# Decoder layer with sparse attention: the first head's bias tile on GpSimd's queue, and filling products that go on past a projection's end

## The chip, the cores and the metric

The kernel runs on one core of one Trainium2 chip. A core has a matrix engine (TensorE, PE in the profile), a vector engine (VectorE, DVE), an activation engine (ScalarE, ACT), GpSimd (POOL) and SyncE (SP). Each works through its own list of instructions in order, and waits for others through semaphores. SP, ACT and POOL also issue transfers (DMA). The metric is the device time of one execution in microseconds (us); lower is better.

## The reference, cut to what matters

One decoder layer on 512 tokens of width 2048 in float32: an attention with three branches, then a gated feed-forward part.

```python
proj = h @ w_in                       # q (16 heads), kc vc ks vs kw vw (4 groups), gates
s_c = q . kcc + bias_c                # compressed keys (31 blocks)
s   = q . kg  + bias                  # selected blocks (with 512 tokens: all of them)
s_w = q . kwb + bias_w                # window of 512
p   = masked_softmax(...)             # each branch
o   = gates0 * o_c + gates1 * o_s + gates2 * o_w
return o.reshape(S, 16 * 128) @ w_out
...
h = h + nsa_mixer(rmsnorm(h), ...)
h = h + swiglu(rmsnorm(h), ffn_w_in, ffn_w_out)
return rmsnorm(h, final_norm_g)
```

The bias depends on the distance of query and key and on the head.

## The kernel before, in words

Every float32 operand is split into a rounded high part and a rest, and each product is three TensorE instructions (`three`, lines 264 to 267). Weights come in granules of 512 KB: a load on SP's queue into one of three `raw` buffers, then a split, high part on ScalarE (line 95), rest on VectorE (line 96), into one of four pairs of buffers. `W.take` hands out the next granule and keeps loads and splits ahead of use.

Three stages follow each other: the first projections with the compression (lines 348 to 625), the attention over 16 heads (lines 628 to 864), and the output projection with the feed-forward part. The change touches the attention.

**The order of one head.** The order of all work is written by hand; each engine gets its instructions in the order in which the code issues them. For each head `h` and block `t` of 128 query tokens, `scores` issues the score products into the one score tile `sc` (three banks of the accumulator memory) and then, per branch, a VectorE instruction that adds the bias and finds the maximum (line 773) and a ScalarE exponential (line 775). The bias of the two long branches is read from the tile `TB[h]`, 128 x 512, one buffer. `finish` scales the result on VectorE. `turn` transposes a piece on TensorE (line 797) into one of two `pt` banks, from which ScalarE and VectorE split it (lines 290, 291), and `values` multiplies it with the values. Blocks are taken from 3 down to 0. Blocks 3 and 2 of the next head are scored at the end of a head.

**The filling products.** TensorE would often wait for the softmax. Between the pieces of a head, `pump(h, step)` therefore issues products of the projections that later heads need: the generator `dense` (lines 711 to 719) goes through queries of two heads (`qpair`), keys and values of the next group (`kpair`, `vpair`), and at the end four pieces of the output projection (`partial`). Each yield of a number is one unit: 650 planned nanoseconds. A projection has 32 units of six (`vpair`) or three instructions, a `partial` 24 of six instructions. It accumulates in two tiles `proj` out of two buffers, so the next projection's first units write where the one before has been read out. After its last unit a projection issues what is left of its read-out, counts itself in `done["n"]`, and yields `None`.

`pump` runs the generator until the planned time reaches a goal that grows with the head and step: one projection of 20,800 planned ns per head up to head 13, and 18,300 per head from there. A head has steps 0 to 11. `drain_to(h + 1)` in heads 0 to 12, between steps 9 and 10, runs it on until the projection that the next head needs is done.

**The first head.** Head 0 has nothing before it, so its blocks 3 and 2 are scored ahead of the loop. The lines are:

```python
load_bias(0)
pump(-1, 9.7)
scores(0, 3)
pump(-1, 10.5)
scores(0, 2)
finish(0, 3)
pump(-1, 11.2)
```

The tiles of the attention lie in memory that the stage before has released. So `TB[0]` and the tiles `P[t]`, whose first columns GpSimd clears (line 635), can be written only when the last readers there are done. The bias comes from `d_u`, a table in device memory that is complete long before. Later heads call `load_bias(h + 1)` within head `h`.

## Time and profile before

| | |
|---|---|
| median of 3 runs | 2159.72 us (2158.61 to 2160.09) |
| profiled execution, its own time | 2158.44 us |
| its span, first to last instruction | 2156.7 us |
| busy in the span: PE / DVE / ACT / POOL | 2136.3 / 1580.3 / 927.9 / 52.8 us |
| granted TensorE clock | 0.998 of full speed |
| attention, about | 196 to 735 us of the span |

The profile is one execution, recorded by the hardware. "Idle before" is the time that an engine stood still before an instruction, with what released it behind the arrow. Matmuls are pipelined: one of 512 columns is shown with 0.39 us, but the next starts some 0.23 us later, so TensorE's instructions overlap in the listing, and a stop shorter than that overlap does not show as idle time. PEld are the weight loads of TensorE. A line number in the profile can be that of a helper: lines 265 to 267 are all products, told apart by their tiles (`proj` filling products, `s` scores, `o` values, `pt` transposes).

### The profile page before, as it was taken

Reading aid. Unit: us, or ns where it says so; the run is one execution under the profiler, and the core shown is the slowest. Engines: PE = TensorE matmul, PEld = TensorE weight load, DVE = VectorE, ACT = ScalarE, POOL = GpSimd, SP = SyncE. Lnnn points to the kernel's source line nnn. Section 1 sums busy time; section 2 is a strip of 40 time slices with the busy share of each in tenths; the row PEclk is TensorE's granted clock in tenths of the full one; section 3 lists DMA queues with packets and bytes.
Section 4 is the critical chain, followed back from the end, with each engine's and each line's share of the span. In section 5 each row is a group of like instructions: output and inputs, shape, how many; then the busy total and the mean of one; then the engine's idle time right before and its main releaser. Section 6 shows DMA issues by size and latency. Waiting matters only on the chain.

```text
span 2156.7 us, 37078 instructions
## 1 busy us (share of the span) xinstructions
PE 2136.3 (99%) x15081; PEld 1983.8 (92%) x15081; DVE 1580.3 (73%) x2616; ACT 927.9 (43%) x1433; POOL 52.8 (2%) x107
## 2 busy tenths in 40 slices
PE   9999999999999999999999999999999999999998
PEld 7898898988989888899999999999999888989996
DVE  5565666665665446898888888888888787877785
ACT  5343454444444224343434434343443454444343
POOL 1000000000000000000000000000000000001000
PEclk9999999999999999999999999999999999999999
DMA  7554322322353543344344434344434686878894
GB/s 227 174 156 138 88 91 82 98 88 84 98 205 103 213 140 107 118 136 129 120 126 128 128 119 126 121 124 128 135 116 131 240 287 215 289 276 308 312 333 143
DMA packets 242727, 344.01 MB, mean 160 GB/s; under 512 B 13259, under 2 KB 179195, under 8 KB 241916
## 3 DMA queue, kind: packets, MB, share of 16 engines
q1 hardware_dynamic: 228412, 272.62, 40.1%
q0 software_dynamic: 12240, 64.82, 7.7%
q10 hardware_dynamic: 1904, 4.20, 0.5%
q8 instruction: 118, 1.93, 0.4%
q14 instruction: 53, 0.43, 0.1%
HBM read 298.50 MB, written 48.34 MB: 161 GB/s over the span
## 4 chain that ended last, share of the span: by engine, by line
PE 97%; DVE 1%; ACT 1%; DMA 1%; issue 0%; SPq 0%; ACTq 0%; DVEq 0%
PE f L266 19%; PE f L267 19%; PE f L265 19%; PE proj L265 8%; PE proj L267 8%; PE proj L266 8%; PE pt L797 2%; PE pp L265 1%; PE pp L266 1%; PE pp L267 1%; PE o L266 1%; PE o L267 1%; PE s L265 1%; PE o L265 1%; PE po L267 1%; PE po L265 1%
## 5 line engine op out<-in xcount | busy, mean ns | idle before, releaser
L96 DVE TENSOR_TENSOR wlo<-raw,whi 128x1024 fp32r<-128x1024 f32 (+1 forms) x226 | 272.3, 1208 | 127.7 <-ACT whi L95 126.2
L95 ACT ACTIVATE whi<-raw 128x1024 fp32r<-128x1024 f32 (+1 forms) x226 | 234.5, 1041 | 222.2 <-DVE raw L954 119.6
L954 DVE TENSOR_TENSOR tlo<-tt,thi 128x1536 fp32r<-128x1536 f32 (+2 forms) x135 | 197.1, 1460 | 110.2 <-ACT thi L1056 88.9
L265 PE MATMUL f<-hn_h,whi 128*128 128x256 f32 x984 | 271.7, 276 | 0.8 <-ACT E L1014 0.8
L267 PE MATMUL f<-hn_h,wlo 128*128 128x256 f32 x984 | 271.6, 276 | 0.0
L266 PE MATMUL f<-hn_l,whi 128*128 128x256 f32 x984 | 271.6, 276 | 0.0
L1051 ACT ACTIVATE whi<-raw 128x1024 fp32r<-128x1024 f32 x123 | 126.0, 1057 | 292.2 <-DVE raw L954 282.0
L265 PE MATMUL proj<-hn_h,whi 128*128 128x512 f32 x512 | 204.4, 399 | 0.5 <-ACT hn_h L400 0.5
L267 PE MATMUL proj<-hn_h,wlo 128*128 128x512 f32 x512 | 200.8, 392 | 0.0
L266 PE MATMUL proj<-hn_l,whi 128*128 128x512 f32 x512 | 199.9, 390 | 0.3 <-DVE hn_l L401 0.3
L265 PEld LDWEIGHTS f<-hn_h,whi 128*128 128x128 f32 x984 | 184.7, 188 | 1.2 <-ACT E L1014 1.2
L267 PEld LDWEIGHTS f<-hn_h,wlo 128*128 128x128 f32 x984 | 184.7, 188 | 0.0
L266 PEld LDWEIGHTS f<-hn_l,whi 128*128 128x128 f32 x984 | 184.7, 188 | 0.0
L1056 ACT ACTIVATE thi<-tt 128x1536 fp32r<-128x1536 f32 x82 | 121.9, 1487 | 84.2 <-PE f L266 84.2
L954 DVE TENSOR_TENSOR wlo<-raw,whi 128x1024 fp32r<-128x1024 f32 x123 | 147.0, 1223 | 0.0
L265 PE MATMUL proj<-whi,hn_h 128*128 128x256 f32 (+2 forms) x496 | 146.3, 295 | 0.0
L267 PE MATMUL proj<-whi,hn_l 128*128 128x256 f32 (+2 forms) x496 | 145.2, 293 | 0.0
L266 PE MATMUL proj<-wlo,hn_h 128*128 128x256 f32 (+2 forms) x496 | 145.0, 292 | 0.0
L291 DVE TENSOR_TENSOR ptl<-pt,pth 128x128 fp32r<-128x128 f32 (+3 forms) x128 | 62.3, 487 | 89.0 <-ACT pth L290 88.9
L267 PE MATMUL f<-whi,tlo 128*128 128x512 f32 x320 | 124.9, 390 | 0.6 <-DVE tlo L954 0.6
L266 PE MATMUL f<-wlo,thi 128*128 128x512 f32 x320 | 125.0, 391 | 0.0
L265 PE MATMUL f<-whi,thi 128*128 128x512 f32 x320 | 124.7, 390 | 0.0
(321 smaller groups left out, 6110.7 us busy)
## 6 DMA issues: line engine op xcount, KB each, us to landing
raw<-in_ffn_w_in SPq DMA_DIRECT2D x135, 512.0 KB, 3.7
raw<-in_ffn_w_out SPq DMA_DIRECT2D x88, 512.0 KB, 5.7
raw<-in_nsa_w_in SPq DMA_DIRECT2D x48, 512.0 KB, 3.8
rawx<-in_ffn_w_in SPq DMA_DIRECT2D x41, 512.0 KB, 4.8
raw<-in_nsa_w_out SPq DMA_DIRECT2D x32, 512.0 KB, 4.0
rawx<-d_a SPq DMA_DIRECT2D x31, 512.0 KB, 4.6
raw<-in_nsa_w_in SPq DMA_DIRECT2D x56, 256.0 KB, 3.4
ah<-d_s POOLq DMA_DIRECT2D x16, 896.0 KB, 6.9
```

Of the source, the lines that this page charges most:

```text
L95: self.nc.scalar.activation(hi[:, :n], src, AF.Copy)
L96: self.nc.vector.tensor_tensor(lo[:, :n], src, hi[:, :n].bitcast(F32), op=OP.subtract)
L265: mm(o, ah, bh, start=start, stop=False, skip_group_check=True)
L266: mm(o, ah, bl, start=False, stop=False, skip_group_check=True)
L267: mm(o, al, bh, start=False, stop=stop, skip_group_check=True)
L291: dve.tensor_tensor(lo, psum_ap, hi.bitcast(F32), op=OP.subtract)
L797: nc.tensor.transpose(pt[rows, 128 * (t - kt):128 * (t - kt + 1)], src, ident)
L954: dve.tensor_tensor(o, a, b, op=OP.subtract)
L1051: act(h, r, AF.Copy)
L1056: act(h, ttf, AF.Copy)
```

## The change

```diff
@@ -726,10 +726,10 @@ def pump(h, step):
             at = h + (step + 4) / STEPS
             goal = 20800 * min(at, 13) + 18300 * max(at - 13, 0)
             while done["ns"] < goal:
-                c = next(stream, None)
-                if c is None:
+                c = next(stream, "end")
+                if c == "end":
                     return
-                done["ns"] += c
+                done["ns"] += c or 0
@@ -744,7 +744,7 @@
         def load_bias(h):
             if h < H:
                 TB[h] = ap_.tile([128, S], F32, name="tb", bufs=1)
-                nc.sync.dma_start(TB[h], bass.AP(tensor=d_u.tensor, offset=d_u.offset + h * UL + 127,
+                (nc.sync if h else pool).dma_start(TB[h], bass.AP(tensor=d_u.tensor, offset=d_u.offset + h * UL + 127,
                                                  ap=[[H * UL - 1, 128], [1, S]]))
```

There are two edits. The bias tile of head 0 alone is loaded on GpSimd's queue instead of SP's; the other 15 stay on SP. And where a projection's end mark (`None`) comes up within a `pump`, the pump no longer returns: it goes on with the first units of the next projection until its goal is reached. It returns early only when all filling products are issued.

## The prediction

> **What bounds the kernel now.** I read the page first: span and engine shares, then busy time and clock by stretch of the attention, and last the order of time around each hole.

> ```profile
> span 2156.7 us, 37078 instructions
> PE 2136.3 (99%) x15081; PEld 1983.8 (92%) x15081; DVE 1580.3 (73%) x2616; ACT 927.9 (43%) x1433; POOL 52.8 (2%) x107
> ```

> ```profile
> core 0: us, PE busy (x) PEld busy (x) DVE busy (x) ACT busy (x) POOL busy (x), PEclk, DMA share, GB/s
> 196.00:207.00 11.00, 11.00 (x56) 9.34 (x55) 5.82 (x7) 3.76 (x5) 0.52 (x4) 1.00 0.42 114
> 207.00:218.00 11.00, 7.68 (x38) 5.78 (x38) 7.20 (x30) 6.20 (x20) 0.00 (x0) 1.00 0.09 22
> 218.00:640.00 422.00, 422.00 (x2517) 371.12 (x2516) 266.59 (x805) 203.40 (x531) 0.00 (x0) 1.00 0.34 104
> 640.00:735.00 95.00, 93.19 (x732) 90.09 (x731) 53.11 (x154) 39.20 (x99) 0.00 (x0) 1.00 0.37 118
> ```

> TensorE carries the time: busy 99%, at a granted clock of 1.00 in every stretch here. The change touches only the attention, from 196 to 735 us, and what it can win there is TensorE's idle time: 11.00 - 7.68 = 3.32 us in the first head, 0 from 218 to 640, 95 - 93.19 = 1.81 at the end. Together 5.13 us, 0.24% of the span. From 218 to 640 TensorE never stands still for as long as the view can show, so there the change can only lose.

> **First head's bias load.** The hole at 207 us, in order of time; here and below only the rows that are used are shown (columns: start, length, engine, line, operation; in brackets the idle time before it):

> ```profile
> 206.70 0.28 PE L267 MATMUL s<-k0h,ql 128*128 128x256 f32 x1
> 207.02 0.19 DVE L773 CUSTOM_DVE_ANT_0 cx<-s,biasc 128x31 f32<-128x31 f32 x1 [1.89 <-PE s L267]
> 207.14 0.08 DVE L773 DVE_READ_ACCUMULATOR2_ANT mx<- 128x1 f32 x1
> 207.97 0.40 PE L267 MATMUL proj<-hn_h,wlo 128*128 128x512 f32 x1
> 208.94 0.69 DVE L773 CUSTOM_DVE_ANT_0 p<-s,tb 128x512 f32<-128x512 f32 x1 [1.72 <-DMA tb<-d_u]
> 210.17 0.08 DVE L773 DVE_READ_ACCUMULATOR2_ANT mx<- 128x1 f32 x1
> 210.31 0.40 PE L265 MATMUL s<-k0h,qh 128*128 128x288 f32 x1 [1.94 <-DVE mx L773]
> 216.79 0.40 PE L265 MATMUL s<-k0h,qh 128*128 128x288 f32 x1 [1.38 <-DVE mx L773]
> ```

> VectorE has the scores of token block 3 and has done the small compressed part by 207.22 (207.14 + 0.08), then waits 1.72 us for the bias tile. TensorE wants the same score banks for block 2; it gets them at 210.31, when VectorE has read them, and stood idle 1.94 us. Why the tile is late:

> ```profile
> 180.77 23.32 SPq L79 DMA_DIRECT2D raw<-in_nsa_w_in  x7
> 204.31 0.34 SPq L747 DMA_DIRECT2D tb<-d_u  x1
> ```

> ```profile
> 196.90 0.52 POOL L635 MEMSET p<- 128x96 f32 x4 [152.58 <-PE tr L622]
> ```

> ```profile
> L747 SPq EVENT_SEMAPHORE  x17: 17/17/28, 204.1 to 666.1; - x17
> L1251 POOL DMA_DIRECT2D acc<-d_r x3: 752/766/768, 1699.4 to 1983.6; - x3
> w<-in_cmp_w_k POOLq DMA_DIRECT2D x1, 128.0 KB, 5.2
> al<-d_s POOLq DMA_DIRECT2D x16, 896.0 KB, 9.2
> ```

> On SP's queue it stands behind weight loads that wait for their buffers, and is issued at 204.31. On GpSimd's queue it stands behind the four clears of `p`, which wait for the last reader of the same released memory (TensorE, line 622) and are over at 196.90 + 0.52 = 197.42. By the code's order nothing else is queued there until the attention is over, so nothing is held up behind the load's waits. The load's own condition is place in that same released region; I take it as met with the clears, at 197.4. The trace bounds this only from above: at 204.1 SP's waits for it took 17 ns, so by then all was free.

> Issue on GpSimd costs 0.77 us of that idle engine. The load has 256 KB; GpSimd's rows nearest to that are 5.2 us (128 KB) and 9.2 (896 KB, queued behind its twin). With 5.2 it lands at 202.6, with 9.2 at 206.6, both before 207.22. VectorE then starts 208.94 - 207.22 = 1.72 us earlier, and block 2's scores can start at 210.31 - 1.72 = 208.59. TensorE's filling products reach that point at 207.97 + 0.23 = 208.20 (0.23 is the distance of two such products, from 18 of them at the join below), so all of the 1.72 counts and 0.39 us of hole stays. What follows, the 1.38 us wait at 216.79 included, is a chain of score, maximum, exponential and weight split with no load in it that lands late, and moves along. I take **-1.72 us**. Other end: place free only at 204.1 and 9.2 us to land gives 213.3, 4.4 us later than 208.94, a loss of **+4.4**. With 5.2 it is 209.3, +0.4.

> SP loses one issue of 0.34 us; its weight loads wait for buffers of the same chain, so that alone gains nothing.

> [...] The trace has a row nearby:

> ```profile
> L1019 POOL DMA_DIRECT2D d_a<-E x22: 532/532/541, 896.8 to 1698.4; - x22
> ```

> ```profile
> 880.00:1700.00 820.00, 818.97 (x7054) 811.64 (x7052) 701.87 (x825) 332.78 (x327) 12.45 (x24) 1.00 0.40 127
> ```

> Twenty-two stores were issued on GpSimd while VectorE was busy 86% of the time (701.87 of 820), each in 532 to 541 ns. [...]

> **Filling products.** Each filling projection is 32 units of 650 planned ns, 20,800 in all, which is one head's share of the plan. So the pump of step 8 ends exactly with a projection's last unit, that of step 9 finds only the end mark and returns with nothing, and that of step 10 makes up with 6 units. Now step 9 gives 3 and step 10 gives 3, in heads 0 to 12. No unit is added or removed. A projection's first three units call for one granule of weights that was split at the end of the one before, so no load, split or eviction changes its place on SP, ACT or VectorE: only TensorE's order changes. In heads 13 to 15 the spill products (24 units) end at steps 7, 5 and 3: there 2, 2 and 1 units come one step earlier, and their residual loads are issued next on SP as before, behind the previous store.

> The join of heads 0 and 1, before:

> ```profile
> 237.47 0.29 PE L265 MATMUL s<-k0h,qh 128*128 128x288 f32 x1
> 238.80 0.28 PE L267 MATMUL s<-k0h,ql 128*128 128x256 f32 x1
> 239.59 0.39 PE L265 MATMUL proj<-hn_h,whi 128*128 128x512 f32 x1
> 243.69 0.29 PE L265 MATMUL s<-k0h,qh 128*128 128x288 f32 x1
> ```

> ```profile
> 233.36 0.68 DVE L317 SCALAR_TENSOR_TENSOR yt<-proj,ybc 128x512 f32<-128x512 f32 x1
> 240.25 0.19 DVE L773 CUSTOM_DVE_ANT_0 cx<-s,biasc 128x31 f32<-128x31 f32 x1
> 241.58 0.08 DVE L773 DVE_READ_ACCUMULATOR2_ANT mx<- 128x1 f32 x1
> 244.96 0.19 DVE L773 CUSTOM_DVE_ANT_0 cx<-s,biasc 128x31 f32<-128x31 f32 x1 [3.29 <-PE s L267]
> ```

> The 18 products from 239.59 to 243.69 take 4.10 us, 0.23 each; nine of them, 2.05 us, move ahead of the scores at 237.47. Do they start at once? Their accumulator was read by VectorE at 233.36 to 234.04, 3.4 us before: yes. Does the second score block still find its banks free at 243.69? The first block's last product moves to 238.80 + 2.05 = 240.85; VectorE begins 0.32 after it (206.70 to 207.02) and reads 1.41 us (240.25 to 241.66), till 242.58, and TensorE could go on 0.06 later (210.25 to 210.31): 242.64. Margin 1.05 us, out of VectorE's idle 3.29, which pays for the delay. The unit count is the same in all these heads, so I cost thirteen joins at **0**. If that cover were gone, each us by which VectorE were later than this margin would cost TensorE one, thirteen times.

> At the end of the last head a hole remains that this edit does meet:

> ```profile
> 703.98 0.68 DVE L706 TENSOR_TENSOR stage<-stage,proj 128x512 f32<-128x512 f32 x1
> 704.68 0.28 PE L267 MATMUL proj<-whi,hn_l 128*128 128x256 f32 x1
> 706.21 0.44 PE L797 MATMUL pt<-ident,p 128*128 128x128 f32 x2 [1.25 <-DVE ptl L291]
> 706.77 0.33 PE L265 MATMUL proj<-whi,hn_h 128*128 128x256 f32 x1
> 709.52 0.28 PE L267 MATMUL proj<-whi,hn_l 128*128 128x256 f32 x1
> ```

> Head 15's step 3 stops at a product's end with one unit; TensorE then waits from about 704.80 to 706.21, 1.4 us, for VectorE to free a bank for transposes. Now one more unit is issued before that wait. The 24 products from 706.77 to 709.52 are 0.12 us apart, so a unit of six is 0.72 us, and its accumulator is free (703.98 + 0.68 = 704.66): **-0.72 us**. Bounds: 0 if that accumulator comes too late, -1.25 if the whole wait went, as the bracket counts it. In heads 13 and 14 the two moved units meet no hole: 0.

> **Sum**, on the profiled execution's own 2158.44 us (span 2156.7 and 1.74 around it): -1.72 + 0 - 0.72 = -2.44, 2156.0 us. The runs' median, 2159.72, is 1.28 above that execution, so the forecast in its terms is **2157.3 us**.

> **Rivals.**
> (1) *A new wait at every join.* The split of a weight granule falls between the two score blocks, on ScalarE and then on VectorE:

> ```profile
> L96 DVE TENSOR_TENSOR wlo<-raw,whi 128x1024 fp32r<-128x1024 f32 (+1 forms) x226 | 272.3, 1208 | 127.7 <-ACT whi L95 126.2
> L95 ACT ACTIVATE whi<-raw 128x1024 fp32r<-128x1024 f32 (+1 forms) x226 | 234.5, 1041 | 222.2 <-DVE raw L954 119.6
> ```

> That is 1.21 + 1.04 = 2.25 us; with the margin of 1.05 gone, TensorE waits 1.20 us thirteen times, 15.6 us: 2157.3 + 15.6 = 2172.9 us. It makes the kernel slower than before from 2.44/13 = 0.19 us a join. For it: 2.05 us of cover really go. Against: in the plan no granule is taken between those units, and the idle 3.29 us stand there. 6%.

> [...] 11%.
> (3) *Gain lost downstream:* a later wait is set by a transfer and does not move, so 2159.7 us. Against: no stretch of the attention shows TensorE waiting for a load. 8%.
> (4) *All of the attention's holes go*, as the earlier start also frees VectorE for the waits behind it: -5.13, 2154.6 us. Against: the 1.38 at 216.79 hangs on VectorE's work itself. 7%.

> **How the numbers follow.** The forecast has the remaining 68%. I call 0.2% (4.3 us) what a measurement of this kernel can tell from no change. Faster by more: rival 4 alone, 0.08 with runs that scatter. Slower by more: rival 1 and the far end of rival 2, 0.08. Within: 0.84. Range: from rival 4 and a little scatter, 2154.5, to rivals 2 and 3 with the runs' own scatter, 2160.6.

> **What would show it.** Bias load on GpSimd's queue near 197.4, landed by 203, and no wait of VectorE for it; the score product of block 2 about 0.4 us after the filling products, and 207 to 218 with 1.6 us of idle TensorE left. At the join, nine products before and nine after the first score block, with VectorE's idle time before the second block down to about 1.2 us and no TensorE wait. In the last head the wait at the transposes down to about 0.7. Wrong if a score product waits for VectorE in heads 1 to 12, or VectorE still waits for the tile at 207.

## The result, and the profile after

| | before | after |
|---|---|---|
| median (range) | 2159.66 us (2158.10 to 2162.06), 18 runs | 2155.57 us (2154.91 to 2156.90), 18 runs |
| ratio to before, 95% interval | | 0.9982 (0.9976 to 0.9988) |
| profiled execution, its own time | 2158.44 us | 2156.00 us |
| its span | 2156.7 us | 2154.3 us |

The medians lie 4.1 us apart, with an interval of 2.6 to 5.2 us (0.0012 and 0.0024 of 2159.66). The two profiled executions lie 2.44 us apart. The forecast was 2157.3 us, 2.44 below the median that was then known.

The page of the changed kernel, and below it busy time and clock in the four stretches that the prediction used:

```profile
span 2154.3 us, 37083 instructions
PE 2137.4 (99%) x15081; PEld 1984.3 (92%) x15081; DVE 1580.8 (73%) x2616; ACT 928.1 (43%) x1433; POOL 53.5 (2%) x108
```

```profile
core 0: us, PE busy (x) PEld busy (x) DVE busy (x) ACT busy (x) POOL busy (x), PEclk, DMA share, GB/s
196.00:207.00 11.00, 11.00 (x54) 9.22 (x53) 6.32 (x10) 3.76 (x5) 1.10 (x5) 1.00 0.44 120
207.00:218.00 11.00, 9.50 (x46) 7.30 (x45) 8.75 (x41) 7.56 (x27) 0.00 (x0) 1.00 0.21 57
218.00:640.00 422.00, 422.00 (x2526) 371.40 (x2526) 266.82 (x801) 203.02 (x528) 0.00 (x0) 1.00 0.33 103
640.00:735.00 95.00, 93.87 (x724) 90.34 (x724) 53.23 (x148) 40.10 (x96) 0.00 (x0) 1.00 0.39 130
```

TensorE's idle time fell from 3.32 to 1.50 us in the first head (11 - 9.50) and from 1.81 to 1.13 us at the end (95 - 93.87). From 218 to 640 it is still 0. The three stretches together have 2.5 us less of it.

The bias load and the score products of head 0, in order of time (start, length, engine, line, operation, idle time before it):

```profile
196.38 0.52 POOL L635 MEMSET p<- 128x96 f32 x4 [152.57 <-PE tr L622]
197.25 0.58 POOL L747 DMA_DIRECT2D tb<-d_u  x1 [0.34 <-issue]
206.50 0.19 DVE L773 CUSTOM_DVE_ANT_0 cx<-s,biasc 128x31 f32<-128x31 f32 x1 [1.89 <-PE s L267]
206.62 0.69 DVE L773 CUSTOM_DVE_ANT_0 p<-s,tb 128x512 f32<-128x512 f32 x1
207.45 0.40 PE L267 MATMUL proj<-hn_h,wlo 128*128 128x512 f32 x1
207.84 0.08 DVE L773 DVE_READ_ACCUMULATOR2_ANT mx<- 128x1 f32 x1
207.97 0.40 PE L265 MATMUL s<-k0h,qh 128*128 128x288 f32 x1
214.44 0.40 PE L265 MATMUL s<-k0h,qh 128*128 128x288 f32 x1 [1.37 <-DVE mx L773]
```

The transfers' view has the landing of this load: one on GpSimd's queue, 256 KB, 3.0 us from issue to landing.

```profile
tb<-d_u POOLq DMA_DIRECT2D x1, 256.0 KB, 3.0
```

So the tile is there at about 200.3, six us before VectorE reads it at 206.62 with no wait in brackets. The scores of block 2 start 0.13 us after VectorE's last read began (207.84 to 207.97). The hole of 1.37 us at 214.44 moved along, as 1.38 had been before.

The join of heads 0 and 1, first TensorE, then VectorE:

```profile
237.19 0.29 PE L265 MATMUL s<-k0h,qh 128*128 128x288 f32 x1
238.49 0.28 PE L267 MATMUL s<-k0h,ql 128*128 128x256 f32 x1
239.29 0.39 PE L265 MATMUL proj<-hn_h,whi 128*128 128x512 f32 x1
241.34 0.29 PE L265 MATMUL s<-k0h,qh 128*128 128x288 f32 x1
```

```profile
238.81 0.19 DVE L773 CUSTOM_DVE_ANT_0 cx<-s,biasc 128x31 f32<-128x31 f32 x1 [0.93 <-PE s L267]
240.15 0.08 DVE L773 DVE_READ_ACCUMULATOR2_ANT mx<- 128x1 f32 x1
242.61 0.19 DVE L773 CUSTOM_DVE_ANT_0 cx<-s,biasc 128x31 f32<-128x31 f32 x1 [2.38 <-PE s L267]
```

The nine products from 239.29 to 241.34 (2.05 us) are what stayed between the score blocks; the other nine come before 237.19. VectorE has read the first block at 240.23, 1.11 us before TensorE writes the next one.

What TensorE still waits for between 200 and 735 us (total, times, longest):

```profile
PE s L265 <- DVE mx L773: 2.0, 3, 1.4
PE pt L797 <- DVE ptl L291: 0.5, 1, 0.5
```

The wait at the transposes of the last head fell from 1.25 to 0.51 us.

### The profile page after: what moved, and what is told of

It is laid out like the page before. It is cut to its first block, busy times and chain, and to the rows that moved or that the text cites. A ratio compares the mean times of both kernels' runs of the same rounds, so it can differ in the third digit from the quotient of the medians.

```text
span 2154.3 us, 37083 instructions
## 1 busy us (share of the span) xinstructions
PE 2137.4 (99%) x15081; PEld 1984.3 (92%) x15081; DVE 1580.8 (73%) x2616; ACT 928.1 (43%) x1433; POOL 53.5 (2%) x108
## 4 chain that ended last, share of the span: by engine, by line
PE 96%; DVE 2%; ACT 1%; DMA 1%; issue 0%; SPq 0%; ACTq 0%; DVEq 0%
PE f L267 19%; PE f L266 19%; PE f L265 19%; PE proj L265 9%; PE proj L267 9%; PE proj L266 8%; PE pt L797 2%; PE pp L267 1%; PE pp L266 1%; PE pp L265 1%; PE o L266 1%; PE o L267 1%; PE s L265 1%; PE o L265 1%; PE s L267 1%; PE s L266 1%
## 5 line engine op out<-in xcount | busy, mean ns | idle before, releaser
L96 DVE TENSOR_TENSOR wlo<-raw,whi 128x1024 fp32r<-128x1024 f32 (+1 forms) x226 | 272.5, 1208 | 127.6 <-ACT whi L95 126.4
L95 ACT ACTIVATE whi<-raw 128x1024 fp32r<-128x1024 f32 (+1 forms) x226 | 234.7, 1041 | 225.8 <-DVE raw L954 122.5
L954 DVE TENSOR_TENSOR tlo<-tt,thi 128x1536 fp32r<-128x1536 f32 (+2 forms) x135 | 197.1, 1460 | 109.7 <-ACT thi L1056 88.7
L265 PE MATMUL f<-hn_h,whi 128*128 128x256 f32 x984 | 271.7, 276 | 0.8 <-ACT E L1014 0.8
L267 PE MATMUL f<-hn_h,wlo 128*128 128x256 f32 x984 | 271.6, 276 | 0.0
L265 PE MATMUL proj<-hn_h,whi 128*128 128x512 f32 x512 | 204.6, 400 | 0.4 <-ACT hn_h L400 0.4
L267 PE MATMUL proj<-hn_h,wlo 128*128 128x512 f32 x512 | 200.9, 392 | 0.0
L265 PEld LDWEIGHTS f<-hn_h,whi 128*128 128x128 f32 x984 | 184.7, 188 | 1.2 <-ACT E L1014 1.2
L267 PEld LDWEIGHTS f<-hn_h,wlo 128*128 128x128 f32 x984 | 184.7, 188 | 0.0
L954 DVE TENSOR_TENSOR wlo<-raw,whi 128x1024 fp32r<-128x1024 f32 x123 | 147.0, 1223 | 0.0
L265 PE MATMUL proj<-whi,hn_h 128*128 128x256 f32 (+2 forms) x496 | 146.4, 295 | 0.0
L267 PE MATMUL proj<-whi,hn_l 128*128 128x256 f32 (+2 forms) x496 | 145.4, 293 | 0.0
L291 DVE TENSOR_TENSOR ptl<-pt,pth 128x128 fp32r<-128x128 f32 (+3 forms) x128 | 62.4, 488 | 89.4 <-ACT pth L290 89.3
L267 PE MATMUL f<-whi,tlo 128*128 128x512 f32 x320 | 124.9, 390 | 0.6 <-DVE tlo L954 0.6
L265 PE MATMUL f<-whi,thi 128*128 128x512 f32 x320 | 124.7, 390 | 0.0
## 6 DMA issues: line engine op xcount, KB each, us to landing
ah<-d_s POOLq DMA_DIRECT2D x16, 896.0 KB, 7.1
```

Source lines behind the costliest of these rows:

```text
L95: self.nc.scalar.activation(hi[:, :n], src, AF.Copy)
L96: self.nc.vector.tensor_tensor(lo[:, :n], src, hi[:, :n].bitcast(F32), op=OP.subtract)
L265: mm(o, ah, bh, start=start, stop=False, skip_group_check=True)
L267: mm(o, al, bh, start=False, stop=stop, skip_group_check=True)
L291: dve.tensor_tensor(lo, psum_ap, hi.bitcast(F32), op=OP.subtract)
L954: dve.tensor_tensor(o, a, b, op=OP.subtract)
```

## The experiments

The sum fits the two profiles and falls 1.7 us short of the medians (4.1 against 2.44). Either the difference is scatter, or the first profile of before shows less of the cost than a usual execution has. The first group takes the edits apart and profiles both kernels again. All ratios are to the kernel before on the same chip.

**The load alone**

```diff
-                nc.sync.dma_start(TB[h], ...
+                (nc.sync if h else pool).dma_start(TB[h], ...
```

> Head 0's bias load on GpSimd's queue, pump as before. Theory A (the prediction's sum holds, -1.72 for the load, and what the medians show beyond -2.44 is scatter of stages that the change does not touch): 1.7 us faster than before, ratio 0.9992, and in the order of time the lead over before is made at one place, between 203 and 209 us. Theory B (the load alone brings most of the 4.1 us of the medians): 3.4 us faster, ratio 0.9984, with a second gain further on. Theory C (the fill brings the excess): 1.7 us, as A.

Measured: 2156.81 us, ratio 0.9987 (0.9978 to 0.9995).

**The pump alone**

```diff
-                c = next(stream, None)
-                if c is None:
+                c = next(stream, "end")
+                if c == "end":
                     return
-                done["ns"] += c
+                done["ns"] += c or 0
```

> The pump that goes on past a projection's end, bias load on SP as before. Theory A: 0.7 us faster, ratio 0.9997, all of it at the transposes near 706 us, the thirteen joins at zero. Theory B: the same 0.7. Theory C (the joins gain, through holes too short to show as idle time): 2.4 us faster, ratio 0.9989, as a lead that grows from head to head between 218 and 640 us.

Measured: 2158.35 us, ratio 0.9994 (0.9985 to 1.0003).

**Both kernels once more, without an edit**

> The changed kernel once more, for a second profile of it. Theory A: the lead over the kernel before is again -1.8 at 209 us and -0.7 at 708, while the offsets at the start (under 30 us) and near 1700 to 1750 us come out different from the first pair of profiles by about 1 us each, since nothing of the change is there. Theories B and C: these offsets come back with the same size and sign. Ratio 0.998 to 0.999.

Measured: 2156.09 us, ratio 0.9984 (0.9975 to 0.9993).

> The kernel before against itself: what a comparison makes of no change, and a second profile of it. Ratio 1.0000, and by theory A its order of time differs from the first profile of it by up to 1 us at the start and near 1700 to 1750 us and nowhere else; by B and C by less than 0.3 us everywhere.

Measured: 2160.04 us, ratio 1.0001 (0.9992 to 1.0010).

**Where each profile gains or loses.** The intervals of these runs are too wide to divide 4 us among two edits: that of the load holds what theory A forecast (0.9992) and what B did (0.9984), that of the pump holds A's 0.9997 and C's 0.9989. The traces do better. All these kernels have the same list of instructions on VectorE, so the same instruction can be looked up in each. The table gives its start minus its start in the first profile of before (us). The rows are times of that profile.

| at | before, 2nd | before, 3rd | after | after, 2nd | load alone | pump alone | pump in heads 13 to 15 |
|---|---|---|---|---|---|---|---|
| 207.0 | +0.03 | -0.36 | -0.52 | -0.21 | -0.49 | -0.57 | -0.25 |
| 220.2 | +1.72 | +0.34 | -2.34 | -2.02 | -2.31 | -0.54 | -0.30 |
| 640.2 | +1.81 | +0.53 | -2.27 | -1.95 | -2.21 | -0.46 | -0.09 |
| 703.7 | +1.96 | +0.65 | -1.95 | -1.81 | -2.05 | -0.25 | +0.04 |
| 711.1 | +1.96 | +0.65 | -2.65 | -2.58 | -2.14 | -0.95 | -0.73 |
| 1740.3 | +2.02 | +0.38 | -2.89 | -2.56 | -2.18 | -1.23 | -0.97 |
| 1750.6 | +3.54 | +1.17 | -1.89 | -1.80 | -1.64 | -0.19 | +1.62 |

A column is read by its steps from row to row. Up to 207 the profiles differ by 0.6 us before the change has done anything. From 207 to 220 the load on GpSimd's queue gains 1.82, 1.81 and 1.82 us over the first profile; with the load on SP's queue the steps are +1.69, +0.70, +0.03 and -0.05. From 220 to 640, with the thirteen joins in it, no profile moves by more than 0.21. From 703.7 to 711.1 the pump gains 0.70, 0.77, 0.70 and 0.77 wherever it is in heads 13 to 15; without it this step is 0.00 to -0.09. So theory C, a lead that grows from head to head, falls. Behind 1740 each profile has a loss of its own over the first, of 0.5 to 2.6 us, whichever kernel it is. Two rows show what it is; the first profile of before, then the pump in heads 13 to 15:

```profile
1743.76 1.06 ACT L1173 ACTIVATE thi<-tt 128x1024 fp32r<-128x1024 f32 x1 [3.71 <-DMA tt<-d_a]
```

```profile
1745.38 1.06 ACT L1173 ACTIVATE thi<-tt 128x1024 fp32r<-128x1024 f32 x1 [6.30 <-DMA tt<-d_a]
```

ScalarE waits there for a transfer that the change doesn't touch, and its wait differs from execution to execution (4.71 in the first profile of after). That is scatter of the runs and no part of the change.

The +1.69 of the second profile of before was in no theory: A had forecast no difference there, B and C under 0.3 us anywhere. The offsets of the two profiles of the changed kernel came out closer together than A had it (0.31 us apart up to 207, 0.24 apart behind 1740, where about 1 us was forecast).

**Why the step of before differs.** The same three rows in the second profile of before, and the stretch behind them in slices of one us:

```profile
204.34 0.34 SPq L747 DMA_DIRECT2D tb<-d_u  x1
210.05 0.69 DVE L773 CUSTOM_DVE_ANT_0 p<-s,tb 128x512 f32<-128x512 f32 x1 [2.80 <-DMA tb<-d_u]
211.42 0.40 PE L265 MATMUL s<-k0h,qh 128*128 128x288 f32 x1 [3.02 <-DVE mx L773]
```

```profile
core 0: us, PE busy (x) PEld busy (x) DVE busy (x) ACT busy (x) POOL busy (x), PEclk, DMA share, GB/s
211.00:212.00 1.00, 0.58 (x4) 0.58 (x5) 0.36 (x2) 1.00 (x3) 0.00 (x0) 0.98 0.00 0
212.00:213.00 1.00, 1.00 (x4) 0.81 (x3) 0.00 (x0) 0.30 (x2) 0.00 (x0) 0.50 0.00 0
214.00:215.00 1.00, 1.00 (x4) 0.79 (x3) 0.86 (x7) 0.94 (x4) 0.00 (x0) 0.50 0.00 0
215.00:216.00 1.00, 1.00 (x7) 0.86 (x6) 1.00 (x3) 1.00 (x3) 0.00 (x0) 0.81 0.00 0
```

The tile came 5.7 us after its issue (204.34 to 210.05), where the first profile has 4.6 (204.31 to 208.94). TensorE stood idle 3.02 us, and from 0.54 us behind that its granted clock was 0.50, from 211.96 to 215.38: 3.42 us, worked out from the slices with 0.98 and 0.81. So the load cost twice: by the hole, and by the lower clock behind it. In the mean clock of the span this is not to be seen: it is 0.998 in the first profile as in this one.

**Twice the load, to make the hole longer**

```diff
+                for _ in range(1 if h else 2):
                     nc.sync.dma_start(TB[h], ...
```

> Kernel before, with head 0's bias tile loaded twice in a row on SP, the second over the first, so that it lands later and the hole at 207 us grows from 1.9 us to some 3 to 6. Theory G (a hole of about 3 us makes the clock gate halve TensorE's clock for one period of 3.41 us, as in the second profile of the kernel before): the profile shows a granted clock of 0.5 for 3.4 us right behind the hole, in nearly every execution, and the time grows by the later landing (about 3.5 us) plus 0.6 to 1.7 us, to 2163.8 us or more, ratio 1.0019 to 1.0025. Theory H (the half clock in that profile was chance and has nothing to do with the hole): clock 1.00 behind the hole, and the time grows by the later landing alone, 2163.2 us or less.

Measured: 2163.37 us, ratio 1.0020 (1.0012 to 1.0029). The hole was 4.59 us, and the clock fell again, as theory G has it (this kernel has one line more ahead of the load and of VectorE's instruction, so their line numbers are one higher):

```profile
203.84 4.94 SPq L748 DMA_DIRECT2D tb<-d_u  x2
211.13 0.69 DVE L774 CUSTOM_DVE_ANT_0 p<-s,tb 128x512 f32<-128x512 f32 x1 [4.38 <-DMA tb<-d_u]
212.49 0.61 PE L265 MATMUL s<-k0h,qh 128*128 128x288 f32 x1 [4.59 <-DVE mx L774]
```

```profile
core 0: us, PE busy (x) PEld busy (x) DVE busy (x) ACT busy (x) POOL busy (x), PEclk, DMA share, GB/s
211.00:212.00 1.00, 0.00 (x0) 0.00 (x0) 0.87 (x3) 0.14 (x1) 0.00 (x0) 0.80 0.00 0
214.00:215.00 1.00, 1.00 (x4) 0.80 (x3) 0.10 (x1) 0.00 (x0) 0.00 (x0) 0.50 0.00 0
217.00:218.00 1.00, 1.00 (x5) 0.90 (x5) 0.62 (x3) 0.86 (x1) 0.00 (x0) 0.50 0.00 0
```

By the slices (0.80 from 211 to 212, 0.50 in each from 212 on) half speed began at 211.60, 0.89 us ahead of the hole's end, and lasted until 218 or longer, at least 6.4 us. Theory G took its hole of about 3 us and its 3.41 us from the second profile of before, where they are 3.02 and 3.42. The time by itself decides less: the ratio is the one that G gave, 2163.37 us lies between the bounds of G and H, and the tile came 2.2 us later than in the first profile of before, not 3.5. That the clock falls with such a hole is shown, at 3.02 and at 4.59 us; that it falls behind the usual one of 1.9 us was still open.

**The kernel before a third time**

> The kernel before once more, for one more profile of its bias load. Four profiles with this load on SP's queue show VectorE waiting 1.72, 2.80, 1.75 and 1.75 us for it. Theory 'late landing is common': a wait of 2.5 us or more, a hole of TensorE of about 3 us, the granted clock at 0.50 for some 3.4 us behind it, and a time of the profiled execution of 2160 us or more. Rival 'the first profile is the usual case': 1.7 to 1.8 us of wait, clock 1.00, about 2158.5 us, and then most of what the medians show beyond 2.44 us is scatter. Ratio 1.0000 in either case.

Measured: 2159.67 us, ratio 1.0002 (0.9993 to 1.0011); the profiled execution took 2159.62 us. Both forms of the expectation missed. The wait was short and the clock fell all the same:

```profile
203.95 0.34 SPq L747 DMA_DIRECT2D tb<-d_u  x1
208.47 0.69 DVE L773 CUSTOM_DVE_ANT_0 p<-s,tb 128x512 f32<-128x512 f32 x1 [1.61 <-DMA tb<-d_u]
209.83 0.41 PE L265 MATMUL s<-k0h,qh 128*128 128x288 f32 x1 [1.82 <-DVE mx L773]
```

```profile
core 0: us, PE busy (x) PEld busy (x) DVE busy (x) ACT busy (x) POOL busy (x), PEclk, DMA share, GB/s
210.00:211.00 1.00, 1.00 (x5) 0.90 (x6) 0.00 (x0) 0.72 (x3) 0.00 (x0) 0.54 0.00 0
211.00:212.00 1.00, 1.00 (x4) 0.81 (x3) 0.00 (x0) 0.00 (x0) 0.00 (x0) 0.50 0.00 0
213.00:214.00 1.00, 1.00 (x5) 0.73 (x4) 0.86 (x6) 1.00 (x5) 0.00 (x0) 0.75 0.00 0
```

Behind a hole of 1.82 us the clock fell, behind one of 1.94 us in the first profile it did not. So the length of the hole alone does not decide. The six profiles with this hole, by its length; the times of the lower clock are worked out from the slices:

| profile | hole, us | from, to | clock behind it | lower clock from, to |
|---|---|---|---|---|
| before, 3rd | 1.82 | 208.01 to 209.83 | 0.50 for 3.42 us | 210.08 to 213.50 |
| pump in heads 13 to 15 | 1.87 | 208.12 to 209.99 | 1.00 | |
| before, 1st | 1.94 | 208.37 to 210.31 | 1.00 | |
| pump alone | 1.97 | 207.80 to 209.77 | 1.00 | |
| before, 2nd | 3.02 | 208.40 to 211.42 | 0.50 for 3.42 us | 211.96 to 215.38 |
| load twice | 4.59 | 207.90 to 212.49 | 0.50 for at least 6.4 us | 211.60 to 218 or later |

Of the four holes between 1.8 and 2.0 us one was followed by a fall, and both longer ones came with one. The falls lie 2.07, 3.56 and 3.70 us after the start of their hole, the last of them within it. At the end of the kernel TensorE has no more work: there the clock was still 1.00 for 1.98 us after the last product in the first profile of before (2146.82 to 2148.80) and for 5.09 us in that of after (2144.89 to 2149.98), and 0.50 from then on. What decides, where the length does not, no run here shows. In the changed kernel the longest hole of head 0 is the 1.37 us at 214.44, and the clock was 1.00 from 196 to 735 us.

**The second edit in the last three heads alone**

```diff
+                if c == "end" or (c is None and h < 13):
                     return
```

> The kernel before with the second edit in heads 13 to 15 alone: no filling products moved at the thirteen joins, the bias load on SP. By the prediction's sum the whole gain of the second edit is the hole at the transposes of the last head: -0.72 us, ratio 0.9997, TensorE's wait there 0.5 to 0.7 us instead of 1.25, and the join of heads 0 and 1 as in the kernel before (VectorE idle 3.29 us before the second score block). Rival 'the joins gain too': no more than about half of the 1.3 us that the second edit alone showed by its medians. The bias load gives one more sample: wait 1.7 to 1.8 or 2.5 and more.

Measured: 2159.06 us, ratio 0.9998 (0.9989 to 1.0007). The wait at the transposes was 0.52 us, and the table above has its step of -0.77 from 703.7 to 711.1. By itself the ratio cannot tell 0.0003 from nothing; the step can. With the joins left as they were (VectorE idle 3.29 us before the second block), nothing of the pump's gain is missing.

**Six units instead of three ahead of the scores**

```diff
-            at = h + (step + 4) / STEPS
+            at = h + (step + (5 if step == 9 and 0 <= h < 13 else 4)) / STEPS
```

Both edits of the change are kept.

> Changed kernel, with all six units of a join issued at step 9, ahead of the first score block, in heads 0 to 12, and none between the two blocks. Theory A (the prediction's margin of 1.05 us at a join, eaten by the 2.05 us of three more units): TensorE waits about 1.0 us for VectorE ahead of the second block in each of 13 heads, 13 us slower than the changed kernel, 2169 us, ratio to before 1.0043. Rival (the margin is larger than read, as the scores could start sooner than the rows suggest, or the wait is made up for later in the head): under 4 us slower, below 2160 us.

Measured: 2173.18 us, ratio 1.0065 (1.0051 to 1.0078). TensorE's waits for VectorE at score products between 218 and 640 us:

```profile
PE s L265 <- DVE mx L773: 10.0, 12, 0.8
```

The thirteenth join lies behind 640:

```profile
647.02 0.40 PE L265 MATMUL s<-k1h,qh 128*128 128x288 f32 x1 [0.83 <-DVE mx L773]
```

TensorE was busy for 411.24 of the 422 us, where the changed kernel has 422.00. Each join has 0.83 us of visible wait. The overlap of products (0.39 us shown, 0.23 to the next) hides another 0.16, so a join costs 0.99, where theory A had about 1.0: the prediction's margin of 1.05 us is real, and three more units use it up. That makes 13 us. Against the changed kernel the ratio rose by 0.0083, some 18 us; where the other 5 come from was not taken apart.

**More units ahead in all heads**

```diff
+            goal += 650 * (4 if h >= 0 else {9.7: 0, 10.5: 1, 11.2: 2}[step])
```

This is added to the changed kernel, to fill the holes at 208 to 215 us; a second kernel has 4 units at the last two pumps ahead of the loop as well and the load on SP's queue.

> Changed kernel, with the pump's goal raised by 1 unit at the second and 2 at the third call ahead of the loop, and by 4 from head 0 on, so that products fill the holes that are left at 208, 210 and 214 us (0.4, 0.2 and 1.4 us). Theory A: up to 2.0 us faster than the changed kernel, 2154 us, ratio to before 0.9974, with TensorE idle for under 0.4 us between 205 and 218. Rival: the places shift at which projections end and weights are split, new waits open elsewhere in the heads, and it is no faster than the changed kernel, 2156 us or more.

Measured: 2162.68 us, ratio 1.0017 (1.0009 to 1.0026). The rival came true.

> The pump as changed and with its goal raised by 4 units from the second call ahead of the loop on, but the bias load on SP as before. Theory A (the load's gain is TensorE's hole at 208 us and nothing else): products fill the hole, so that the load's place no longer matters, and the time is that of the kernel with the same goals and the load on GpSimd, within 1 us. Rival (the load on SP costs something else, a weight load behind it or a later chain): 1.7 us or more slower than that kernel.

Measured: 2164.43 us, ratio 1.0026 (1.0015 to 1.0037). With the load on GpSimd's queue the holes were gone, but each later head had a new wait:

```profile
core 0: us, PE busy (x) PEld busy (x) DVE busy (x) ACT busy (x) POOL busy (x), PEclk, DMA share, GB/s
205.00:218.00 13.00, 13.00 (x68) 11.00 (x67) 8.88 (x41) 7.84 (x27) 0.00 (x0) 1.00 0.23 62
218.00:640.00 422.00, 418.60 (x2479) 364.92 (x2478) 259.81 (x771) 199.64 (x512) 0.00 (x0) 1.00 0.33 103
```

From 218 to 640 TensorE waits for VectorE at a score product once per head, twelve times and 3.4 us in all. Against the changed kernel the ratio rose by 0.0035, 7.6 us, so these waits are less than half of it. With the shift kept over all heads, the weight granules are split at other places of every head. That these splits make VectorE read the scores later fits the rows, but was not taken apart.

With the load on SP's queue, VectorE still waited 1.75 us for the tile, and the products did fill the hole behind that. But TensorE then waited 1.02 us at 214.35, one block later (11.98 of the 13 us up to 218 were busy), and the medians lie 1.75 us apart, as the rival has it, though with intervals that overlap. The two kernels also differ in the goals of the two pumps ahead of the loop, so this difference is not the queue's alone.

**More units ahead in head 0, given back within it**

```diff
+            goal += 650 * {(-1, 10.5): 1, (-1, 11.2): 2, (0, 0): 3, (0, 1): 2, (0, 2): 1, (0, 3): 1}.get((h, step), 0)
```

Again in the changed kernel; the second form has 1, 2, 4, 3, 3, 2, 2, 1, 1.

> The changed kernel with up to 3 filling units issued earlier within head 0 (1, 2, 3, 2, 1, 1 units ahead at the two pumps before the loop and steps 0 to 3, none from step 4 on), so that later heads keep their order. It aims at the hole of 1.37 us at 214.4 and the two of some 0.3 us at 208 and 210.5. Theory 'a hole of VectorE's chain can be filled where it is, if the order of the other heads stays': from 205 to 218 us at most 0.4 us without TensorE work instead of 1.5, 422.00 of 422 busy after it, 2154.4 us, ratio 0.9976, 0.0006 below the changed kernel's. Rival 'the units are missed where they are taken from': the holes come back at steps 1 to 4 of head 0 or the third weight granule, split one step earlier, makes a product wait; 2155.6 us or more, ratio 0.9982.

Measured: 2154.14 us, ratio 0.9977 (0.9968 to 0.9986).

> As the run before, but with 4 units ahead at step 0 and given back one at a time until step 7 (1, 2, 4, 3, 3, 2, 2, 1, 1), so that no step of head 0 has less than one unit; two granules are split one step earlier. Theory as before: no hole of TensorE from 205 to 218, 2154.1 us, ratio 0.9974. Rival 'the earlier splits on ScalarE and VectorE delay the softmax of head 0': a product waits for VectorE in head 0 by 0.3 to 1.0 us, 2155 us, ratio 0.9980. If this one is slower than the shorter one, the splits decide; if faster, the number of units does.

Measured: 2154.69 us, ratio 0.9979 (0.9970 to 0.9988). The stretches of the shorter form:

```profile
core 0: us, PE busy (x) PEld busy (x) DVE busy (x) ACT busy (x) POOL busy (x), PEclk, DMA share, GB/s
205.00:218.00 13.00, 12.84 (x68) 10.66 (x68) 9.16 (x43) 7.90 (x28) 0.00 (x0) 1.00 0.23 60
218.00:640.00 422.00, 422.00 (x2532) 371.69 (x2531) 268.41 (x809) 203.88 (x534) 0.00 (x0) 1.00 0.33 105
```

The hole of 1.37 us came down to 0.16, and the later heads keep their 422.00. The first profile of before has the same VectorE instruction at 300.4 us; the shorter form is 4.15 ahead of it there and the changed kernel 2.33, with starts that differ by less than 0.1 up to 207. So it gains 1.8 us over the changed kernel inside head 0. The longer form gains 0.5 more between 207 and 300 (from -0.06 to -4.09, against -0.59 to -4.15) and is busy for all of the 13 us up to 218, so its earlier splits did no harm there. The times of the two forms, and theirs against the changed kernel's 0.9982, lie within each other's intervals, so the further gain is shown by the traces and not by the times.

## Why the prediction was right or wrong

The direction, the mechanism and the size of each step in the profile came out as forecast; what was too small is the amount that the kernel before usually loses.

**The bias load, -1.72.** Its place was free when GpSimd had cleared `p` (issue at 197.25, forecast near 197.4), it landed before 203, and VectorE's wait went. Of the 3.32 us of idle time in this head 1.50 stayed (forecast 1.6). Against the first profile the step is 1.82, where 1.72 was worked out. The mis-sized term is this one all the same: it was read from one execution and put on the median unchanged. The prediction took the 1.28 us between that execution and the median as an offset that both kernels share. In five profiles with the load on SP's queue (three of before, two with only the pump edited) the stretch from 207 to 220 took 0, 1.69, 0.70, 0.03 and -0.05 us more than in the first. The mean is 0.47, so the load is worth about 1.82 + 0.47 = 2.3 us, and up to 3.5 where the tile is late and the clock falls. The part that the prediction lacked is the granted clock behind the hole, 0.50 for 3.42 us in two of the five. It had read 1.00 in the one profile there was, with a hole of 1.94 us.

**The joins, 0.** Right: no wait of a score product from 218 to 640 us, no step in the table, and a margin of 1.11 us where 1.05 was worked out. One detail differs. VectorE's idle time before the second block is 2.38 us and not about 1.2. In the kernel before VectorE was late for the first block (it began 240.25 - 238.80 = 1.45 us after the last product); now it is waiting for it (0.93) and begins 0.32 after it. So over 1.1 of the 2.05 us that moved came out of this lateness. Rival 1 (a wait at every join) fell; the run with six units shows that it was one step away.

**The end of the last head, -0.72.** Measured 0.70 to 0.77, with 0.51 us of the wait left (forecast 0.7).

**The other rivals.** Rival 2 (tile as late as before) fell: 0.58 us to issue, 3.0 to land, while VectorE was busy 2.25 of 3.10 us (197.2 to 200.3). Its 11%, its part in the upper end of the range and in the chance of slower were the author's estimate for a tile that comes as late on GpSimd's queue. No run shows such a tile; in the profiles of after, of its repeat and of the load alone it was issued between 197.2 and 197.6 and landed 2.9 to 3.0 us later. Rival 3 (a later transfer takes the gain) fell: in the three profiles with the load on GpSimd's queue the lead at 220 is still there at 703.7, but for 0.2 to 0.4 us. Rival 4 (all holes go) fell as well, since the 1.37 us at 214.44 stayed; it needs the added units of the last experiments.

**The sum.** About 2.3 for the load and 0.7 for the end give 3.0 us, inside the measured 2.6 to 5.2. That the two profiled executions lie just the forecast 2.44 apart is luck: up to 1750 us the column of the changed kernel also has -0.52, +0.39, -0.24 and +1.00 at places where the change does nothing, and some -0.5 follows; these nearly cancel. That the median lies inside the range is in part luck as well, as its lower end was set for rival 4, which fell.

The medians of this comparison show 4.1 and those of its repeat 3.6 (2159.66 - 2156.09), which leaves 0.6 to 1.1 us that the profiles don't place. More late tiles than one in five, or more lowered clocks than two in five, would be enough. The mean clock of most timed runs is on record, and that bears on the second. Half speed at the kernel's end, 4.3 us in the profile of after and 7.9 in the first of before, takes 0.0010 and 0.0018 off this mean, and one stretch of 3.42 us at half speed takes another 0.0008. If the ends of the timed runs lie between these two, a run at 0.999 has no such stretch in front of its end, and one at 0.997 or less has one. Of 40 runs with the load on GpSimd's queue (the changed kernel and the load alone), 31 are at 0.999 and none is below 0.998. Of 110 runs of the kernel before, 41 are at 0.999 and 12 at 0.997 or less. If a run without such a stretch reads 0.999 as often in both, about half of the runs of before had one (an estimate from these counts). That is little more than two in five, so most of the rest stays open.

## What to carry to other kernels

A hole read from one profile is one sample: before its size goes into a sum, ask whether what ends it is a transfer that lands at varying times (here 4.5 to 5.7 us after its issue), and look at the granted clock in short slices behind it, not at the mean (here 0.50 for 3.42 us, in a mean of 0.998). An idle queue can take a load out from behind weight loads that wait for buffers; here that cost 0.58 us of an engine that was otherwise idle. Filling work may move past a dependent pair of steps only within the reader's spare time there (here 2.05 us moved at no cost and 4.10 us cost 0.83 us of visible wait at a join), and where it is moved for one place it is best given back nearby: here it cost 7.6 us when kept up over all heads, and gained 1.8 us in the trace when given back within the first.

## What the runs showed of the hardware

The same 256 KB came 4.5 to 5.7 us after their issue on SP's queue (204.31 to 208.94, 204.34 to 210.05, 203.95 to 208.47), among the weight loads of the first head, and in 2.9 to 3.0 us on GpSimd's queue some seven us earlier, when the DMA engines had less to do (columns as above):

```profile
197.20:200.30 3.10, 3.10 (x15) 2.59 (x14) 2.25 (x3) 1.08 (x2) 0.58 (x1) 1.00 0.34 91
204.30:209.00 4.70, 4.07 (x21) 3.15 (x19) 0.95 (x4) 0.52 (x3) 0.00 (x0) 1.00 0.62 171
```

The first row is the load on GpSimd's queue in the changed kernel: a DMA share of 0.34, and 91 GB/s, which over 3.1 us is little more than the 256 KB of this load. The second is the first profile of before: a share of 0.62. Which part of the difference is the queue and which the moment was not taken apart.
